# Two pairs' A12 block products remade as seven inner quarter products in the projection stage of a hybrid attention block

## The chip, the core and the metric

The kernel runs on one core of a Trainium2 chip. The metric is device time in microseconds for one execution. TensorE (PE) does the matmuls; its weight loads (PEld) overlap them. VectorE (DVE), ScalarE (ACT) and GpSimd (POOL) work on tiles in SBUF, DVE and ACT also on PSUM; SyncE (SP) issues most transfers. Each engine takes its instructions in program order.

## What is computed

One layer of a block with three parallel mixers. Nearly all of its arithmetic is matrix products in float32 with a model width of 1024 and 1024 tokens:

```python
h = rms_norm(x, g_pre)
a_qkv, bq, bk, bv, mq, ga, gb, gm, mg = split(h @ w_in)   # w_in: 1024 x 10496 columns
aq, ak = rope(a_qkv[0], pos), rope(a_qkv[1], pos)         # dilated windows, 3 groups of 8 heads
...                                                       # three attentions
ya = (oa * silu(ga)) @ w_br_a                             # and yb, ym
gates = sigmoid(mg + b_merge)
out = (gates[0] * ya + gates[1] * yb + gates[2] * ym) @ w_out
x + rms_norm(out, g_post)
```

The change lies in the part of `h @ w_in` that makes the rotated queries and keys of the dilated attention (`aq`, `ak`), some of the SiLU gates, and the merge gates (`mg`).

## The kernel before

**Precision.** A float32 operand is held as two tiles, a high part (`h`) that ACT rounds to PE's format and a low part (`l`) that DVE computes as the difference; the helper `split` (lines 90 to 92) does both. A product of two operands is three matmuls: high by high, high by low, low by high. In the matmul rows of the profile, 128*128 is the weight tile and 128x512 the moving one.

**Pairs and blocks.** The stage around line 1370 takes two units of 128 output columns at a time, called a pair: 27 pairs, numbered by `n` in the order of `PAIRS` (line 1097): rope units and others (three of SiLU gates, twelve of merge gates) in turn, so that pairs 0, 2, ... 22 are rope, 1, 3, 5 gates, and 7, 9, ... 23, 24, 25, 26 merge. The 1024 inner dimension and the 1024 tokens are each halved, and the two units are the third halving: a pair is a 2 by 2 block product, which the kernel makes with seven block products instead of eight, after Strassen and Winograd. The blocks of the weights are A11, A12 (first unit: first and second half of the inner dimension), A21, A22 (second unit) and four sums of them, S1 to S4; those of the tokens are B11 to B22 and four sums T1 to T4. `PRODUCTS` (line 954) says which goes with which:

```python
PRODUCTS = (("A11","B11"), ("A12","B21"), ("S2","T2"), ("S3","T3"), ("S4","B22"), ("S1","T1"), ("A22","T4"))
```

Each block product is 12 matmuls of 128x512 (four inner chunks by three terms), in `pair_product`. The tokens' blocks are made before the stage and lie in tiles `hh`, `hl` and others; the weights' sums are made on POOL by `k_sum` (S1, S2, S3, S4 are its `j` 1, 2, 3, 4, in three tiles `SF`, named vot, vot, vgt), and split by `k_block` into four tiles vS in turn. A11 and A12 are split together by `k_own` into one pair of tiles `OWN` (wh, wl), 1024 columns wide.

**What follows a product.** Products accumulate in PSUM: X (A11, then S2, S3, A22 on top), W (S1, then S4) and Y (A12). Between them ACT copies X out (`keep_copy`: after A11 to `p1`, after S2 to `v_`, after S3 to `y_`), so a later product into X has to wait for the copy. `c_add` adds a PSUM bank and such a copy on DVE, which gives a quarter of the pair's result: unit `u`, token half `t`. `c_fin` scales it (merge, gate: one DVE operation and later, by `behind`, Tanh on ACT and a store) or multiplies it by cosine and sine (rope: two DVE operations); `turn_it` combines rope results on POOL into tiles ko (L1213, L1214), and `k_store` stores them.

**Order.** It is written out by hand in the loop over `n` (lines 1458 to 1529): PE runs, for each pair, S2(n), S1(n), S3(n), A11(n+1), A22(n), A12(n+1), S4(n), and behind each product stand the DVE, ACT, POOL and DMA instructions that are issued with it. Each engine keeps this order and waits only for data and for tiles that come free. `k_load` loads a unit's weights (512 KB, on SP) two pairs ahead. The stage before (line 1340) makes the values of the third group in the same block form with 128x256 matmuls; its side work stands in the table `SIDE`, whose keys are its 28 steps.

Of the kernel before, what the change touches and what calls it, by code (L numbers as in the profile page):

```python
# [33 lines left out]
def block(ctx: ExitStack, tc: tile.TileContext, x, xT, memT, cst, msk, bcst, tabA, gpost,  # L34
# [224 lines left out]
    wos = dram.tile([3, 4, P, S], F32, name="wos")  # L259

# [911 lines left out]
    def c_fin(n, u, t, ps_=None):  # L1172

        r = RV.pop((n, u, t)) if ps_ is None else kr() if n < last else p1
# [107 lines left out]
    for n in range(28):  # L1282
# [34 lines left out]
        if k == 3:  # L1317
            left += [lambda i=i, j=j, b=now[j]: v_evac(i, j, b) for j in range(4)]

    SIDE = {2: [lambda: v3_sum("S2", "A22", "S3", OP.subtract, v3.tile([P, 1024], F32, name="xS2"))],  # L1320
# [41 lines left out]
    close(v3p)  # L1362
    kpp, kp = pool("kp")
    p1, v_, y_ = [vb.tile([P, 512], F32, name=x) for x in ("vv2", "vv3", "vrt")]
    SPARE = [wp.tile([P, 1024], F32, name=x) for x in ("wh", "wl")]
# [4 lines left out]
    def pair_product(n, an):  # L1370
# [5 lines left out]
        for k in range(4):  # L1376
            bh, bl = k_tokens(TOKENS[an], k)
            for q, (a, b) in enumerate(((ah[:, k], bh), (ah[:, k], bl), (al[:, k], bh))):
                PE.matmul(BANK[n, c], a, b, start=k == 0 and q == 0 and not more, stop=k == 3 and q == 2,  # L1379
                          skip_group_check=c in "XW")  # L1380

# [76 lines left out]
    for n in range(last + 1):  # L1458
        N = n + 1
        pair_product(n, "S2")  # L1460
        c_add(*((n - 1, 0, 1, BANK[n - 1, "W"], v_) if n else (0, 0, 0, BANK[0, "Y"], p1)))
        behind()
        k_block(n, "A22")
        if n == last:
            y_load(1)
        if n:
# [7 lines left out]
        behind()  # L1474
        if n < last:
            k_own(N)
        if n:
# [6 lines left out]
        pair_product(n, "S3")  # L1484
        behind()
# [4 lines left out]
        if n + 2 <= last:  # L1490
            k_load(n + 2, 0)
        if n == last - 1:
            op_load(lo)
        c_fin(n, 0, 0)
# [4 lines left out]
        behind()  # L1499
        if n < last:  # L1500
# [37 lines left out]
    behind()  # L1538
    close(kpp)
# [900 lines left out]
```

## Time and profile before

| | |
|---|---|
| median of 3 runs | 1362.17 us (1361.77 to 1362.71) |
| the profiled execution | 1362.23 us, span 1360.5 us |
| PE busy | 98% of the span, granted clock 0.998 |
| DVE, ACT, POOL busy | 74%, 48%, 43% |
| DMA | 213.84 MB, mean 157 GB/s |
| pair stage | 527.1 to 1041.7 us of the span, 2268 matmuls |

A row of the profile begins with a line of the kernel, the engine and the operation; then come the tiles written and read, with numbers left out, and shapes. In rows in order of time the first two numbers are start and duration in microseconds, and brackets at the end give idle time of the engine just before and what ended it. The idle time of an engine that is not the bound costs nothing by itself.

### The profile page before, as it was taken

How to read it: one execution, taken by the hardware profiler on the slowest of the kernel's cores; microseconds unless marked ns; L12 is line 12 of the kernel's file. 1: busy time of each engine (PE TensorE's matmuls, PEld its weight loads, DVE VectorE, ACT ScalarE, POOL GpSimd, SP SyncE). 2: the span in 40 equal slices, each digit the busy share in tenths (PEclk: the TensorE clock that was granted, in tenths of full speed). 3: DMA queues.
4: the chain of work that ended last, by engine and by line, in shares of the span. 5: the costliest groups of instructions: out<-in, count | busy, mean ns of one | idle time of the engine just before them, and what ended most of it. 6: DMA issues, size and time to landing. Idle time of an engine off the chain costs nothing.

```text
span 1360.5 us, 23348 instructions
## 1 busy us (share of the span) xinstructions
PE 1338.4 (98%) x8567; PEld 1101.6 (81%) x8567; DVE 1011.6 (74%) x1821; ACT 650.4 (48%) x1383; POOL 588.8 (43%) x449
## 2 busy tenths in 40 slices
PE   7999999999999999999999999999999999999997
PEld 7899987767668899888888888888888777778886
DVE  7868677776776877777887766787756666768977
ACT  7544366666654443333334333333345676763332
POOL 0516703778760003455556534565531244662003
PEclk9999999999999999999999999999999999999999
DMA  6356522223157773232333333332256777977455
GB/s 254 109 171 232 180 94 93 82 82 113 62 171 273 241 237 130 85 111 90 124 116 111 122 108 124 117 109 99 90 174 229 248 219 230 274 229 234 145 186 185
DMA packets 124435, 213.84 MB, mean 157 GB/s; under 512 B 31680, under 2 KB 63776, under 8 KB 124320
## 3 DMA queue, kind: packets, MB, share of 16 engines
q1 hardware_dynamic: 115008, 198.42, 44.5%
q10 hardware_dynamic: 9312, 13.93, 2.8%
q8 instruction: 67, 1.10, 0.3%
q14 instruction: 48, 0.39, 0.1%
HBM read 145.92 MB, written 66.38 MB: 156 GB/s over the span
## 4 chain that ended last, share of the span: by engine, by line
PE 91%; DVE 3%; ACT 2%; DMA 1%; issue 1%; POOL 1%; SPq 0%; DVEq 0%; ACTq 0%; POOLq 0%
PE s L1379 38%; PE d L1978 6%; PE s L1290 4%; PE ov L866 4%; PE s L2202 4%; PE sc L2120 3%; PE s L1340 3%; PE s L1653 2%; PE d L133 2%; PE d L131 2%; PE d L129 2%; PE s L848 2%; PE s L849 2%; PE tr L830 2%; PE d L572 2%; PE d L2202 2%
## 5 line engine op out<-in xcount | busy, mean ns | idle before, releaser
L1379 PE MATMUL s<-hh,vS 128*128 128x512 f32 x432 | 141.6, 389 | 0.0
L854 POOL TENSOR_TENSOR bl<-bl,bp 128x512 f32<-128x512 f32 x90 | 118.4, 1316 | 35.3 <-ACT bp L851 29.4
L1379 PE MATMUL s<-vA,vS 128*128 128x512 f32 x486 | 114.5, 389 | 0.0
L92 DVE TENSOR_TENSOR vS<-vot,vS 128x512 fp32r<-128x512 f32 x81 | 92.3, 1141 | 20.1 <-ACT vS L91 20.1
L1379 PEld LDWEIGHTS s<-vA,vS 128*128 128x128 f32 x486 | 91.2, 188 | 18.9
L831 DVE TENSOR_REDUCE bn<-tr 128x1 f32<-128x512 f32 x128 | 83.9, 687 | 23.8 <-PE tr L830 22.5
L851 ACT ACTIVATE bp<-s 128x512 f32<-128x512 f32 x128 | 76.3, 598 | 40.7 <-PE s L849 36.9
L1379 PEld LDWEIGHTS s<-hh,vS 128*128 128x128 f32 x432 | 81.1, 188 | 16.8
L1379 PE MATMUL s<-hh,wl 128*128 128x512 f32 x216 | 84.3, 390 | 0.0
L1379 PE MATMUL s<-hl,wh 128*128 128x512 f32 x216 | 84.1, 389 | 0.0
L1379 PE MATMUL s<-hh,wh 128*128 128x512 f32 x216 | 84.1, 389 | 0.0
L1379 PE MATMUL s<-hl,vS 128*128 128x512 f32 x216 | 84.0, 389 | 0.0
L1665 ACT ACTIVATE pra<-pra,sts 128x192 f32<-128x192 f32 (+1 forms) x176 | 72.4, 415 | 14.5 <-DVE sts L1664 14.2
L1124 POOL TENSOR_TENSOR vot<-wr 128x512 f32<-128x512 f32 x14 | 23.9, 1707 | 117.0 <-DMA wr<-in_wu 115.6
L1383 ACT ACTIVATE vv<-s 128x512 f32<-128x512 f32 x54 | 32.3, 599 | 87.9 <-PE s L1379 55.7
L1664 DVE CUSTOM_DVE_ANT_0 pra<-s,mask 128x192 f32<-128x192 f32 (+1 forms) x192 | 48.8, 309 | 33.6 <-PE s L1653 19.4
L133 PE MATMUL d<-hh,wl 128*128 128x512 f32 x160 | 64.0, 400 | 0.0
L131 PE MATMUL d<-hl,wh 128*128 128x512 f32 x160 | 63.4, 397 | 0.0
L129 PE MATMUL d<-hh,wh 128*128 128x512 f32 x160 | 62.9, 393 | 0.0
L1124 POOL TENSOR_TENSOR vot<-vot,vA 128x512 f32<-128x512 f32 x13 | 20.9, 1609 | 94.0 <-DVE vS L92 94.0
L866 PE MATMUL ov<-bp,VS 128*64 128x256 f32 x512 | 58.8, 382 | 0.0
L91 ACT ACTIVATE vS<-vot 128x512 fp32r<-128x512 f32 x81 | 49.4, 625 | 12.2 <-ACT vy L1191 4.1
(640 smaller groups left out, 4007.4 us busy)
## 6 DMA issues: line engine op xcount, KB each, us to landing
wr<-in_wu SPq DMA_DIRECT2D x38, 512.0 KB
vA<-in_wu SPq DMA_DIRECT2D x26, 512.0 KB
qkd<-ko SPq DMA_DIRECT2D x96, 128.0 KB
wl<-thd SPq DMA_DIRECT2D x24, 512.0 KB
wos<-os SPq DMA_DIRECT2D x12, 512.0 KB
wr<-in_wbr SPq DMA_DIRECT2D x24, 256.0 KB
aq<-qkd SPq DMA_DIRECT2D x12, 512.0 KB
ak<-qkd SPq DMA_DIRECT2D x12, 512.0 KB
```

The source lines that it names most:

```text
L92: V.tensor_tensor(dst_l, src, dst_h.bitcast(F32), op=OP.subtract)
L129: PE.matmul(dst, wh[:, k, :], hh[k][:, t], start=k == 0, stop=False)
L131: PE.matmul(dst, wh[:, k, :], hl[k][:, t], start=False, stop=False)
L133: PE.matmul(dst, wl[:, k, :], hh[k][:, t], start=False, stop=k == 7)
L831: V.tensor_reduce(st[i]["n"][:, j, c:c + 1], s, axis=AX.X, op=OP.min)
L851: A.activation(pp, s, AF.Exp, scale=-1.0)
L854: E.tensor_tensor(lsum[i % 2], d[0] if kt == 1 else lsum[i % 2], pp, op=OP.add)
L866: PE.matmul(o[e * 64:e * 64 + 64, c].rearrange("p (j q) -> p j q", j=2), w, x[:, e], start=kt == 0, stop=kt == NT, skip_group_check=True)
L1379: PE.matmul(BANK[n, c], a, b, start=k == 0 and q == 0 and not more, stop=k == 3 and q == 2, skip_group_check=c in "XW")
L1665: A.activation(src, src, AF.Exp, scale=-1.0, bias=bias, accum_out=sts[:, 1, h, T:T + 1])
L1978: PE.matmul(ps_, a, b, start=k == 0 and q == 0, stop=k == 3 and q == 2)
L2202: PE.matmul(dst[:, e[0]:e[1]], a, b, start=k == 0 and q == 0, stop=k == 3 and q == 2)
```

## The change

The second weight block times the first token half of the second half of the inner dimension, A12 by B21, leaves the sequence of single pairs. Pairs (1, 2), (3, 4) to (25, 26) are taken together: their two A12 blocks, stacked, are a matrix of 256 output columns by 512, B21 is 512 by 512 tokens, and this product is itself made by seven inner products of quarter blocks in the same scheme, each of six 128x256 matmuls (`q_product`). Only pair 0 keeps its own A12 product.

- PE: 312 matmuls of 128x512 go, 546 of 128x256 come. In an odd pair the inner A11, A12 stand behind S2, the inner S2 behind S3, the inner S1 behind A22; in the even pair behind it the inner S3 stands behind S2, the inner A22 and S4 behind S1. They accumulate in two PSUM banks of another pool and one of the stage's.
- DVE: seven `q_add` per two pairs add the 256-column results from PSUM into `P1[0]` and `P1[1]`, copies of X after A11; the first quarters of both pairs (`c_fin(.., 0, 0)`) are finished together in the even pair, and their two `c_add` go. `k_own` splits 512 columns; the other half of `OWN` holds A12 of the odd pair's inner blocks, split by `k_own_second` in the even pair ahead, and then inner S3 and A22, split by `q_last`. `q_blocks` splits the inner S1, S2, S4 into tiles na and nb.
- POOL: `q_sums`, four 256-column sums per two pairs, behind `k_sum(N, 2)`.
- SP: `q_load`, four loads of 512 KB per two pairs of the token sums (two tiles nt in turn). `k_load(n + 2, 0)` stands earlier in the loop.
- Ahead of the stage, steps 3 to 17 of the stage at line 1340 get `QUARTER_STEPS`: four loads of xT, four scalings on ACT, eight sums, four splits on ACT and POOL, four stores to a new DRAM tensor `tqd`.
- `c_add(n, 1, 1)` stands ahead of A22(n) and `behind` after `k_own`. The program is built with a smaller scratch for descriptors, which frees SBUF.

On DVE, from the scaled quarter of the even pair 8 to the add that frees W's copy. vS tiles are blocks of weights, s and d PSUM, tab the rope tables, vy, vv, wh, wl results in spare tiles. Before:

```order
L1170 TENSOR_TENSOR vv_7199<-s_7126,vrt 128x512
L1197 TENSOR_TENSOR vy_7215<-s_7026,tab_5514 128x512
L1198 TENSOR_TENSOR vv_7214<-s_7026,tab_5515 128x512
L92 TENSOR_TENSOR vS_7218<-vot,vS_7218 128x512
L1170 TENSOR_TENSOR vy_7233<-s_7201,vv_5954 128x512
L92 TENSOR_TENSOR vS_7235<-vot,vS_7235 128x512
L92 TENSOR_TENSOR vS_7238<-vgt,vS_7238 128x512
L1170 TENSOR_TENSOR wh<-s_7126,vv_5955 128x512
```

and now:

```order
L92 TENSOR_TENSOR wl<-vA_7183,wh 128x512
L1176 TENSOR_TENSOR vy_7414<-s_7341,vrt 128x512
L1203 TENSOR_TENSOR vy_7443<-s_7233,tab_5515 128x512
L1204 TENSOR_TENSOR vv_7442<-s_7233,tab_5516 128x512
L92 TENSOR_TENSOR vS_7446<-vot,vS_7446 128x512
L92 TENSOR_TENSOR na<-vy_7419,na 128x512
L92 TENSOR_TENSOR nb<-vv_7420,nb 128x256
L92 TENSOR_TENSOR vS_7465<-vot,vS_7465 128x512
L92 TENSOR_TENSOR vS_7468<-vgt,vS_7468 128x512
L1176 TENSOR_TENSOR vy_7502<-s_7341,vv_5993 128x512
```

The add for the quarter (0, 0) of pair 9 is gone from between S2(9) and S1(9), two inner splits stand there instead, and the second half of `OWN` is split ahead of the add.

On POOL, the same period: sums into vot and vgt for the blocks of pair 9 (and the next pair's first), and the two turns of pair 8 into ko. Before:

```order
L1124 TENSOR_TENSOR vot<-vot,vA_7023 128x512
L1124 TENSOR_TENSOR vot<-vA_7023,vot 128x512
L1213 TENSOR_TENSOR ko_7242<-vy_7166,vv_7214 128x16x32
L1214 TENSOR_TENSOR ko_7243<-wl,vy_7215 128x16x32
L1124 TENSOR_TENSOR vot<-wr 128x512
```

and now:

```order
L1125 TENSOR_TENSOR vot<-vot,vA_7183 128x512
L1439 TENSOR_TENSOR vy_7419<-wr 128x256
L1440 TENSOR_TENSOR vy_7419<-vy_7419,vA_7183 128x256
L1441 TENSOR_TENSOR vv_7420<-vA_7183,vy_7419 128x256
L1442 TENSOR_TENSOR vv_7420<-vA_7183,wr 128x256
L1125 TENSOR_TENSOR vot<-vA_7183,vot 128x512
L1219 TENSOR_TENSOR ko_7472<-wl,vv_7442 128x16x32
L1220 TENSOR_TENSOR ko_7473<-wl,vy_7443 128x16x32
```

The four quarter sums stand between the sum for S2(9) and the sum for S4(9).

The diff, cut to its core:

```diff
+    tqd = dram.tile([4, P, S], F32, name="tqd")
...
-        split(h, l, KR[n, 0])
+        t = slice(0, 512 if n else S)
+        split(h[:, t], l[:, t], KR[n, 0][:, t])
...
+    def k_own_second(n):
+        h, l = OWN
+        split(h[:, hi], l[:, hi], KR[n, 0][:, hi])
...
+    def q_load(nm):
+        nc.sync.dma_start(q_tile(nm).bitcast(F32), tqd[int(nm[1]) - 1])
...
+    def q_sums(a):
+        x, y = QS[a] = [kr(), kr()]
+        G.tensor_tensor(x[:, 0:256], rows_at(a + 1, 0), rows_at(a + 1, 1), op=OP.add)
+        G.tensor_tensor(x[:, 256:512], x[:, 0:256], rows_at(a, 0), op=OP.subtract)
+        G.tensor_tensor(y[:, 0:256], rows_at(a, 1), x[:, 256:512], op=OP.subtract)
+        G.tensor_tensor(y[:, 256:512], rows_at(a, 0), rows_at(a + 1, 0), op=OP.subtract)
+
+    def q_blocks(a):
+        x, y = QS[a]
+        split(NX[0][:, 0], NX[0][:, 1], x)
+        split(NX[1][:, 0, 0:256], NX[1][:, 0, 256:512], y[:, 0:256])
+
+    def q_last(a):
+        h, l = OWN
+        split(h[:, 768:1024], l[:, 768:1024], QS.pop(a)[1][:, 256:512])
+        split(h[:, 512:768], l[:, 512:768], rows_at(a + 1, 1))
...
+        for k in range(2):
+            m = slice(128 * k, 128 * k + 128)
+            bh, bl = b[k]
+            for q, (u, x) in enumerate(((w[0][:, m], bh), (w[0][:, m], bl), (w[1][:, m], bh))):
+                PE.matmul(QB[c], u, x, start=first and k == 0 and q == 0, stop=k == 1 and q == 2, skip_group_check=True)
+
+    def q_add(z, t, c):
+        x = P1[z][:, 256 * t:256 * t + 256]
+        V.tensor_tensor(x, QB[c], x, op=OP.add)
...
+        one, two, ahead = n % 2 == 1, n > 0 and n % 2 == 0, N % 2 == 1 and n < last
         pair_product(n, "S2")
+        if one:
+            q_product("A11")
+            q_product("A12")
         c_add(*((n - 1, 0, 1, BANK[n - 1, "W"], v_) if n else (0, 0, 0, BANK[0, "Y"], p1)))
+        if one:
+            q_add(0, 0, "X")
+            q_add(0, 0, "Y")
+        elif two:
+            q_add(1, 1, "W")
+            q_product("S3")
+            q_add(1, 1, "X")
         behind()
         k_block(n, "A22")
...
+        if n + 2 <= last:
+            k_load(n + 2, 0)
...
         pair_product(n, "S1")
         keep_copy(v_, n)
-        behind()
+        if two:
+            q_product("A22")
+            q_product("S4")
+            q_add(1, 0, "X")
+            q_add(0, 1, "W")
         if n < last:
             k_own(N)
+        behind()
...
         pair_product(n, "S3")
+        if one:
+            q_product("S2")
+            q_add(0, 1, "X")
+            q_load("T3")
...
-        c_fin(n, 0, 0)
+        if not n:
+            c_fin(n, 0, 0)
+        elif two:
+            for z in range(2):
+                c_fin(n - 1 + z, 0, 0, P1[z], P1[z] if n == last else None)
+        if ahead:
+            k_own_second(N)
...
+        c_add(n, 1, 1, BANK[n, "W"], y_)
...
+        if one:
+            q_last(n)
+        if ahead:
+            q_sums(N)
+            for nm in ("T2", "T1"):
+                q_load(nm)
         pair_product(n, "A22")
         if n < last:
-            keep_copy(p1, N)
-        c_add(n, 1, 1, BANK[n, "W"], y_)
+            keep_copy(P1[N % 2 == 0], N)
...
-        pair_product(N, "A12")
+        if one:
+            q_product("S1")
+            q_load("T4")
         c_fin(n, 1, 0, BANK[n, "X"])
         k_block(N, "S2")
+        if ahead:
+            q_blocks(N)
...
         pair_product(n, "S4")
-        c_add(N, 0, 0, BANK[N, "Y"], p1)
...
-    nc = bacc.Bacc("TRN2", target_bir_lowering=False, num_devices=1)
+    nc = bacc.Bacc("TRN2", target_bir_lowering=False, num_devices=1, dynamic_dma_scratch_size=1024)
```

More of the change, by code (lines that the diff above doesn't have):

```diff
@@ L1170, in c_add, with c_fin @@
         V.tensor_tensor(r, ps_, z, op=OP.add)
[L1172 to L1174 removed]
+    def c_fin(n, u, t, ps_=None, r=None):
+        r = RV.pop((n, u, t)) if ps_ is None else r or (kr() if n < last else SF[1])
         src = r if ps_ is None else ps_
@@ L1329, in block @@
             26: [lambda: k_block(0, "S2")], 27: [lambda: k_block(0, "S1"), lambda: k_block(0, "S3"), lambda: k_sum(0, 4)]}
+    QUARTER_STEPS = {3: [lambda: [q_source(i) for i in range(4)]], 5: [lambda: [q_scale(i) for i in range(2)]],
+                     6: [lambda: [q_scale(i) for i in range(2, 4)]], 7: [lambda: q_sub("T3", "B22", "B12")],
+                     8: [lambda: q_sub("T1", "B12", "B11")], 9: [lambda: q_split("T3")],
+                     11: [lambda: q_sub("T2", "B22", "T1")], 12: [lambda: q_split("T1")],
+                     14: [lambda: q_sub("T4", "B21", "T2")], 15: [lambda: q_split("T2")], 17: [lambda: q_split("T4")]}
     for n in range(28):
@@ L1353, in block @@
         for f in SIDE.get(n, ()):
+            f()
+        for f in QUARTER_STEPS.get(n, ()):
             f()
@@ L1380, in pair_product, with rows_at, q_product @@
                           skip_group_check=c in "XW")
+    def rows_at(n, z):
+        return KR[n, 0][:, 512 + 256 * z:768 + 256 * z]
+    QS = {}
+    def q_sums(a):
[12 more added lines that the diff above has]
+        split(h[:, 512:768], l[:, 512:768], rows_at(a + 1, 1))
+    QB = {}
+    def q_product(an):
+        i = ("S1", "S2", "S4").index(an) if an in ("S1", "S2", "S4") else None
+        if i is None:
+            c = 512 if an in ("A11", "A22") else 768
+            w = [x[:, c:c + 256] for x in OWN]
+        else:
+            w = [NX[0][:, z, 256 * i:256 * i + 256] if i < 2 else NX[1][:, 0, 256 * z:256 * z + 256] for z in range(2)]
+        bn = TOKENS[an]
+        if bn[0] == "T":
+            t = TQ[bn].rearrange("p (x k q) -> p x k q", x=2, k=2)
+            b = [(t[:, 0, k], t[:, 1, k]) for k in range(2)]
+        else:
+            kk, t = 2 + 2 * int(bn[1]), slice(256 * int(bn[2]) - 256, 256 * int(bn[2]))
+            b = [(hh[kk + k][:, t], hl[kk + k][:, t]) for k in range(2)]
+        c = "Y" if an == "A12" else "W" if an in ("S1", "S4") else "X"
+        first = an in ("A11", "A12", "S1")
+        if first:
+            QB[c] = (pss1() if c == "Y" else psd())[:, 0:256]
+        for k in range(2):
+            m = slice(128 * k, 128 * k + 128)
[5 more added lines that the diff above has]
+        V.tensor_tensor(x, QB[c], x, op=OP.add)
     def keep_copy(dst, n):
@@ L1489, in block @@
             k_sum(N, 3)
-        if n + 2 <= last:
-            k_load(n + 2, 0)
         if n == last - 1:
             op_load(lo)
-        c_fin(n, 0, 0)
+        if not n:
+            c_fin(n, 0, 0)
+        elif two:
+            for z in range(2):
+                c_fin(n - 1 + z, 0, 0, P1[z], P1[z] if n == last else None)
+        if ahead:
+            k_own_second(N)
         if n == last:
@@ L1538, in block @@
     behind()
+    close(nqp)
     close(kpp)
```

34 lines of the change are left out of this document (30 added, 4 removed).

## Prediction

> **What bounds the kernel now.** I read the shares of the engines first, then the chain that ended last, then the pair stage by windows, then the order of time of DVE, POOL and ACT in one period of it. From the page:
>
> ```profile
> PE 1338.4 (98%) x8567; PEld 1101.6 (81%) x8567; DVE 1011.6 (74%) x1821; ACT 650.4 (48%) x1383; POOL 588.8 (43%) x449
> PE 91%; DVE 3%; ACT 2%; DMA 1%; issue 1%; POOL 1%; SPq 0%; DVEq 0%; ACTq 0%; POOLq 0%
> ```
>
> PE is the bound nearly everywhere. Two windows price a matmul (length, PE busy and count, PEld, clock, DMA share); the third is one period of two pairs with all engines (PE, PEld, DVE, ACT, POOL). Below them stand the first and last matmul of the pair stage, and what PE's weight loads waited for in it (us, times).
>
> ```profile
> 527.10:1041.70 514.60, 514.60 (x2268) 425.15 (x2268) 1.00 0.36 117
> 486.70:527.10 40.40, 40.35 (x336) 40.28 (x336) 1.00 0.62 199
> 674.00:712.10 38.10, 38.10 (x169) 31.38 (x168) 30.30 (x31) 14.27 (x22) 21.34 (x12) 1.00 0.35 111
> 527.06 0.40 PE L1379 MATMUL s<-hh,wh 128*128 128x512 f32 x1
> 1041.38 0.39 PE L1379 MATMUL s<-hh,vS 128*128 128x512 f32 x1
>   DVE wl L92: 0.8, 4
> ```
>
> A 128x512 matmul costs 514.60/2268 = 0.2269 us, a 128x256 one in the stage before 40.35/336 = 0.1201 us. A product of a pair is 12 matmuls, 2.72 us; product number k of the stage (A11(0) is 0, then A12(0), then seven per pair) starts at 527.06 + 2.7225k. So A11(9) is product 61 and starts at 693.14, A22(8) ends at 698.58, S2(9) starts at 704.0, S3(9) at 709.5. PE hardly waits, yet DVE has only 38.1 - 30.3 = 7.8 us idle in a period, and the one wait shown is for a DVE split: DVE is close behind.
>
> **The change: PE.** 26 A12 products leave, 26 x 12 x 0.2269 = 70.8 us. 13 x 7 inner products of six 128x256 matmuls come, 546 x 0.1201 = 65.6 us. The difference is -5.2 us, -0.40 per period. The 256-wide rate is measured with a new weight load for each matmul, as here, and PEld was busy all the time there too (40.28 of 40.40), so I see no further bound.
>
> The Trainium skill (TensorE: Matmul & The Clock Gate, Back-to-back issue gap) gives N/2.4 + 2.5 ns for the isolated gap, 215.8 and 109.2 ns, and by that the saving would be an estimated 7.7 us. The rows' two rates are slower, so the sum goes by them.
>
> **The change: what must now be hidden.** Per period DVE gets seven 256-wide PSUM adds for two 512-wide ones, seven splits (four of 512, three of 256 columns) for two of 1024; POOL gets four 256-wide sums; ACT the high halves; SP four 512 KB loads. The question is when, so I walk one period, the even pair 8, a rope pair, in the clock of before. DVE, before (start, duration, what it waited for):
>
> ```profile
> 691.02 1.23 DVE L92 TENSOR_TENSOR wl<-vA,wh 128x1024 fp32r<-128x1024 f32 x1 [2.26 <-ACT wh L91]
> 692.17 0.69 DVE L1178 TENSOR_TENSOR vy<-vy,rb 128x512 f32<-128x512 f32 x1
> 694.73 0.69 DVE L92 TENSOR_TENSOR vS<-vot,vS 128x512 fp32r<-128x512 f32 x1 [1.87 <-ACT vS L91]
> 695.34 0.69 DVE L1197 TENSOR_TENSOR vy<-wl,tab 128x512 f32<-128x512 f32 x1
> 696.06 1.67 DVE L1198 TENSOR_TENSOR wl<-wl,tab 128x512 f32<-128x512 f32 x1
> 697.65 0.68 DVE L1170 TENSOR_TENSOR vv<-s,vrt 128x512 f32<-128x512 f32 x1
> 698.80 0.69 DVE L1197 TENSOR_TENSOR vy<-s,tab 128x512 f32<-128x512 f32 x1 [0.48 <-PE s L1379]
> 699.41 0.68 DVE L1198 TENSOR_TENSOR vv<-s,tab 128x512 f32<-128x512 f32 x1
> 700.01 0.68 DVE L92 TENSOR_TENSOR vS<-vot,vS 128x512 fp32r<-128x512 f32 x1
> 701.52 0.69 DVE L1170 TENSOR_TENSOR vy<-s,vv 128x512 f32<-128x512 f32 x1 [0.83 <-PE s L1379]
> 702.13 2.50 DVE L92 TENSOR_TENSOR vS<-vot,vS 128x512 fp32r<-128x512 f32 x1
> 704.55 2.57 DVE L92 TENSOR_TENSOR vS<-vgt,vS 128x512 fp32r<-128x512 f32 x1
> 707.04 0.68 DVE L1170 TENSOR_TENSOR wh<-s,vv 128x512 f32<-128x512 f32 x1
> ...
> 711.17 1.22 DVE L92 TENSOR_TENSOR wl<-wr,wh 128x1024 fp32r<-128x1024 f32 x1
> ```
>
> POOL in the same period, the two turns of pair 12 (another dilation group), and the mean of a 256-wide POOL operation:
>
> ```profile
> 695.57 1.61 POOL L1124 TENSOR_TENSOR vot<-vot,vA 128x512 f32<-128x512 f32 x1 [7.35 <-DVE vS L92]
> 700.77 1.29 POOL L1124 TENSOR_TENSOR vot<-vA,vot 128x512 f32<-128x512 f32 x1 [3.59 <-DVE vS L92]
> 702.02 2.06 POOL L1213 TENSOR_TENSOR ko<-vy,vv 128x512 f32<-128x512 f32 x1
> 704.02 2.55 POOL L1214 TENSOR_TENSOR ko<-wl,vy 128x512 f32<-128x512 f32 x1
> ...
> 778.24 1.29 POOL L1213 TENSOR_TENSOR ko<-vy,wh 128x512 f32<-128x512 f32 x1
> 779.48 1.74 POOL L1214 TENSOR_TENSOR ko<-vv,wl 128x512 f32<-128x512 f32 x1
> ```
>
> ```profile
> L356 POOL TENSOR_TENSOR qn<-t1b,ssb 128x256 f32<-128x256 f32 x16 | 10.8, 678 | 1.3
> ```
>
> ACT:
>
> ```profile
> 692.94 0.72 ACT L1191 ACTIVATE vy<-vy,cs 128x512 f32<-128x512 f32 x1 [1.95 <-DVE vy L1178]
> 693.69 0.33 ACTq L1192 DMA_DIRECT2D thd<-vy  x1
> 694.06 0.63 ACT L91 ACTIVATE vS<-vot 128x512 fp32r<-128x512 f32 x1 [0.40 <-ACT vy L1191]
> ...
> 707.82 0.60 ACT L1383 ACTIVATE vv<-s 128x512 f32<-128x512 f32 x1 [2.94 <-DVE wh L1170]
> ```
>
> The reader should see that a split of SBUF operands takes 0.61 us to the next start when POOL is idle (700.01), but 2.50 and 2.57 us beside the turns: it started at 702.13, POOL's turn ended at 704.08, it ended 0.55 us later; and POOL's next operation in turn got longer by that. The two take turns, whole operations at a time; operations that read PSUM (707.04) stay at 0.6. The SBUF — State Buffer page of the Trainium skill (Who interferes with whom) says the same, an exclusive lock for a whole instruction; by it the new POOL sums, all SBUF to SBUF, speak against this change.
>
> The walk after. The last inner product in front of S3(8), S4, ends one product ahead of A11(9), at 690.41; DVE, in order, waits for it with its add, so it is idle until 690.63 (0.22 behind the end, as 698.80 behind 698.58). Add 0.34, half split of the next pair 0.6, scaling of pair 7 at 691.57 (before 692.17). From that scaling to the S4 split lie 2.56 us, as in before (692.17 to 694.73: Tanh, its store, the high half, all on ACT): 694.13. Then in queue order, POOL in brackets: split 694.73; the scaling of pair 7 that moved here, 695.4; [sum for S2(9), 1.16, that is 1.61 less its wait for DVE]; first rope operation of pair 8; [quarter sum 0.58, my estimate from 0.68 and half of 1.16]; second rope operation; [quarter sum]; second half of the OWN split: 699.4; PSUM add 699.95; two PSUM rope operations 701.17 (before 700.01); S2(9) split 701.8. S2(9) now starts one product earlier than before, at 701.3, its low block is used 0.23 later: 0.35 us late.
>
> Next, two inner-block splits with [S2(9) released, sum 1.2] between them: 703.9; [turn 2.0], S1(9) split 706.4; [turn 2.0], S3(9) split 708.9; the W add 709.6; the copy of X on ACT 0.7, as from 707.04 to 708.42 in before: 710.3. S3(9) on PE may not start before that copy. PE's own way to S3(9) from 698.58 is S4, S2, two inner products and S1, 9.6 us: 708.2. So S3(9) waits 2.1 us, the 0.35 included. The margin in before was 709.5 - 708.4 = 1.1. The first half of OWN for A11(10) ends about 713.6 and is needed at 714.0 behind that wait: covered.
>
> Bounds: if no POOL operation held DVE here, the walk is shorter by 1.16 + 1.16 + 1.2 + 4.0 = 7.5 us and the wait is nothing; if every one of the four quarter sums and both sums for pair 10 held it too, 3.5 us more, a wait of 5.6. I take 2.1, since the rows show the alternation exactly. The rest is nearer zero: in the odd pair the same walk ends some 0.5 us ahead of PE; the quarter sums of tokens in the stage before (POOL about 10 us more) lie beside DVE that is idle at 494 to 516 and splits that are used microseconds later: 0, if that cover fails about 1 us; four loads more raise the DMA share from 0.35 by about 2 MB in 38 us, 55 GB/s beside 111: 0. Two loads wait on SP for inner products, with the stores of the rotated tiles behind them; these have a period's time. The inner products accumulate in two banks that this stage leaves idle and in one of its six; before took three new ones per pair, now five per two pairs.
>
> **Sum.** Pairs 4, 6, 8, 10, 16, 18, 20, 22 have the long turn: 8 x 2.1 = 16.8. Of these pairs 4 and 6 also have a gate's extra DVE pass in the moved steps: 2 x 0.6 = 1.2. Pairs 2, 12, 14 have the short turn (1.2 each, 1.6 us less): 3 x 0.5 = 1.5. The last two periods have no turn: 0. With PE's -5.2: +14.3. The profiled execution took 1362.23 us (span 1360.5), 0.06 above the median of 1362.17: 1376.5.
>
> **Rivals.** The gain arrives: PE stays full, 1362.2 - 5.2 = 1357. For it: PE waited only 0.8 us in 514.6, and DVE has 7.8 us of idle time per period. It needs the walk to S3(9) to be 2.1 us shorter, for instance if one turn of 2.0 us ran while DVE reads PSUM; from there on the time is below before. Against it: that walk is a single chain in queue order, and the margin of before was 1.1 us while PE's way there got 1.3 us shorter.
>
> Half of it: the quarter sums run beside PSUM operations only and the 0.35 and 1.2 us fall away, leaving 0.9 us in eight periods, 1362.2 + 7 - 5 + 1 = 1365, just slower.
>
> DVE becomes the bound of the whole period: 30.3 + 7 of new work and POOL's 2.6 us of sums, against 37.7 of PE; with the upper bound of 5.6 us in eight periods, 1362 + 45 - 5 = 1402. The idle time at 690 speaks against it.
>
> Late token quarters (T3, T4 are loaded only after the inner product before has let go): some 9 us from issue to use, for one 512 KB load at 111 GB/s and more; a late microsecond in 12 periods gives 1369.
>
> **Chances.** Walk as above (1370 to 1385) 0.51; gain 0.19; half 0.19, of which a third within the resolution; DVE bound 0.07; late loads 0.04. About 0.2% is what a measurement can tell from no change (1359.4 to 1364.9). Faster 0.18, same 0.08, slower 0.74. The likeliest case's own range is 1370 to 1385; the range to hold eight in ten goes from the gain, 1356.5, to 1386.
>
> **What would show it.** Right: PE waits in the even pairs ahead of S3, for ACT's copy, behind the DVE add on W; DVE splits of 1.5 to 2.6 us beside POOL; the 256-wide matmuls at 0.120 us; periods near 39.8 us with long turns, near 38.2 with short ones. Wrong: periods of 37.7 us without waits, or waits for the loads of the token quarters, or a 256-wide rate above 0.13 us, which alone would eat the gain.

## The result, and the profile after

The changed kernel took **1397.32 us** (median of 4, 1396.45 to 1399.87) against 1362.44 (1361.77 to 1362.97) for the kernel before beside it: ratio 1.0259, 95% interval 1.0244 to 1.0275. Slower, as forecast, but by 34.9 us where +14.3 was forecast, and above the range of 1356.5 to 1386. The profiled execution of after took 1399.87 us, its span 1398.0. The shares of the engines and the chain that ended last, from the page of after:

```profile
PE 1346.6 (96%) x8801; PEld 1111.9 (80%) x8801; DVE 1084.9 (78%) x1951; ACT 668.4 (48%) x1456; POOL 651.0 (47%) x513
PE 44%; DVE 14%; ACT 2%; DMA 2%; issue 1%; POOL 0%; ACTq 0%; DVEq 0%; POOLq 0%
```

PE's share of the chain fell from 91% to 44%, DVE's rose from 3% to 14%. PE's own waits in the two stages, longest first (engine, line, whom it waited for: us, times, longest). L1382 is the stage ahead of the pairs, L1429 a pair's product, L1176 `c_add`, L1485 `keep_copy` (in other kernels these numbers differ a little):

```profile
PE s L1429 <- DVE vy L1176: 7.8, 6, 2.4
PE s L1382 <- ACT wh L91: 5.1, 2, 4.6
PE s L1429 <- DVE wl L1176: 5.1, 3, 2.5
PE s L1429 <- ACT vv L1485: 4.4, 6, 3.1
PE s L1429 <- DVE wh L1176: 3.8, 2, 2.5
PE s L1382 <- DVE wl L92: 2.3, 3, 1.1
```

So there are two losses: one in the stage ahead, which had no such wait, and one in the pairs, mostly for `c_add` and not for ACT's copy. By windows (length; busy time and count of PE, PEld, DVE, ACT, POOL; clock; DMA share; GB/s) the two stages and one long-turn period of two pairs, from S4(8) to S4(10):

```profile
487.40:538.00 50.60, 43.17 (x338) 42.02 (x338) 29.36 (x36) 20.08 (x31) 12.75 (x13) 0.93 0.65 206
538.00:1079.80 541.80, 518.96 (x2505) 432.44 (x2504) 458.58 (x550) 210.29 (x376) 313.47 (x209) 0.99 0.49 163
725.21:764.92 39.71, 38.25 (x186) 31.86 (x186) 35.09 (x41) 15.32 (x28) 25.28 (x17) 1.00 0.48 159
```

The stage ahead took 50.6 us where it had taken 40.4, the pair stage 541.8 where it had taken 514.6: 10.2 and 27.2, together 37.4 of the 37.5 by which the span grew. In order of time, the wait in the period of pair 10 (PE), with DVE, ACT and POOL around it:

```profile
764.92 0.50 PE L1429 MATMUL s<-hh,vS 128*128 128x512 f32 x1 [1.30 <-DVE vy L1176]
756.41 0.69 DVE L1184 TENSOR_TENSOR vy<-vy,rb 128x512 f32<-128x512 f32 x1
758.99 0.69 DVE L92 TENSOR_TENSOR vS<-vot,vS 128x512 fp32r<-128x512 f32 x1 [1.89 <-ACT vS L91]
759.60 0.68 DVE L1184 TENSOR_TENSOR vy<-vv,rb 128x512 f32<-128x512 f32 x1
760.20 1.78 DVE L1206 SCALAR_TENSOR_TENSOR vv<-nc,tab 128x512 f32<-128x512 f32 x1
761.91 1.22 DVE L1207 SCALAR_TENSOR_TENSOR vv<-nc,tab 128x512 f32<-128x512 f32 x1
763.05 1.22 DVE L92 TENSOR_TENSOR wl<-vA,wh 128x512 fp32r<-128x512 f32 x1
764.19 0.68 DVE L1176 TENSOR_TENSOR vy<-s,vrt 128x512 f32<-128x512 f32 x1
768.62 2.56 DVE L92 TENSOR_TENSOR vS<-vot,vS 128x512 fp32r<-128x512 f32 x1
773.57 0.68 DVE L1176 TENSOR_TENSOR wl<-s,vv 128x512 f32<-128x512 f32 x1
757.20 0.72 ACT L1197 ACTIVATE vy<-vy,cs 128x512 f32<-128x512 f32 x1 [3.02 <-DVE vy L1184]
758.32 0.63 ACT L91 ACTIVATE vS<-vot 128x512 fp32r<-128x512 f32 x1 [0.40 <-ACT vy L1197]
759.83 1.60 POOL L1125 TENSOR_TENSOR vot<-vot,vA 128x512 f32<-128x512 f32 x1 [7.57 <-DVE vS L92]
763.80 1.05 POOL L1441 TENSOR_TENSOR wh<-vA,vy 128x256 f32<-128x256 f32 x1
```

S4(10) accumulates on W, so it may not start before `c_add(n, 1, 1)` has read W (764.19). In before A12 of the next pair, 2.72 us, stood between A22 and S4 and covered that; now nothing does. Ahead of the add DVE stood idle for 1.89 us: the split for S4 wants ACT's high half (758.32), ACT is in order and first does the tanh of pair 9 (757.20), and that wants DVE's product (756.41). The walk I had forecast is otherwise there.

### The profile page after: what moved, and what is told of

Same layout as the page of the kernel before. It is cut to its first block, busy times and chain, and to the rows that moved or that the text cites. A ratio compares the mean times of both kernels' runs of the same rounds, so it can differ in the third digit from the quotient of the medians.

```text
span 1398.0 us, 24177 instructions
## 1 busy us (share of the span) xinstructions
PE 1346.6 (96%) x8801; PEld 1111.9 (80%) x8801; DVE 1084.9 (78%) x1951; ACT 668.4 (48%) x1456; POOL 651.0 (47%) x513
## 3 DMA queue, kind: packets, MB, share of 16 engines
q8 instruction: 69, 1.13, 0.3%
## 4 chain that ended last, share of the span: by engine, by line
PE 44%; DVE 14%; ACT 2%; DMA 2%; issue 1%; POOL 0%; ACTq 0%; DVEq 0%; POOLq 0%
PE s L1429 19%; PE d L2116 6%; DVE vS L92 4%; PE s L2340 4%; PE d L1478 3%; PE sc L2258 3%; PE s L1791 2%; PE d L2340 2%; DVE wl L92 2%; PE tr L1857 1%; PE tr L1825 1%; DVE nb L92 1%; DMA tqd<-nt 1%; DVE vy L1184 1%; ACT vS L91 0%
## 5 line engine op out<-in xcount | busy, mean ns | idle before, releaser
L1429 PE MATMUL s<-hh,vS 128*128 128x512 f32 x432 | 144.5, 396 | 18.1 <-DVE vy L1176 7.8
L855 POOL TENSOR_TENSOR bl<-bl,bp 128x512 f32<-128x512 f32 x90 | 118.8, 1320 | 34.9 <-ACT bp L852 29.0
L1429 PE MATMUL s<-vA,vS 128*128 128x512 f32 x486 | 119.8, 393 | 1.6 <-ACT vv L1485 1.3
L1429 PEld LDWEIGHTS s<-hh,vS 128*128 128x128 f32 x432 | 81.8, 189 | 40.4 <-DVE vy L1176 10.4
L1429 PEld LDWEIGHTS s<-vA,vS 128*128 128x128 f32 x486 | 88.2, 188 | 21.1 <-ACT vv L1485 5.0
L832 DVE TENSOR_REDUCE bn<-tr 128x1 f32<-128x512 f32 x128 | 84.0, 687 | 24.7 <-PE tr L831 23.3
L92 DVE TENSOR_TENSOR vS<-vot,vS 128x512 fp32r<-128x512 f32 x81 | 86.5, 1074 | 21.3 <-ACT vS L91 21.3
L1429 PE MATMUL s<-hl,vS 128*128 128x512 f32 x216 | 84.7, 392 | 0.0
L1485 ACT ACTIVATE vv<-s 128x512 f32<-128x512 f32 x41 | 24.5, 598 | 100.1 <-PE s L1429 32.1
L92 DVE TENSOR_TENSOR wl<-wr,wh 128x1024 fp32r<-128x1024 f32 (+2 forms) x39 | 50.2, 1287 | 22.8 <-ACT wh L91 22.8
L91 ACT ACTIVATE vS<-vot 128x512 fp32r<-128x512 f32 x81 | 50.6, 626 | 11.6 <-ACT vy L1197 3.7
L849 PE MATMUL s<-QH,KS 128*128 128x512 f32 x128 | 52.6, 411 | 1.5 <-ACT bp L852 1.5
L867 PEld LDWEIGHTS ov<-bp,VS 128*64 128x64 f32 x512 | 35.3, 137 | 21.9 <-issue 5.4
L831 PE MATMUL tr<-KS,QH 128*128 128x512 f32 x128 | 52.3, 408 | 0.1
```

Source lines behind the costliest of these rows:

```text
L92: V.tensor_tensor(dst_l, src, dst_h.bitcast(F32), op=OP.subtract)
L832: V.tensor_reduce(st[i]["n"][:, j, c:c + 1], s, axis=AX.X, op=OP.min)
L855: E.tensor_tensor(lsum[i % 2], d[0] if kt == 1 else lsum[i % 2], pp, op=OP.add)
L867: PE.matmul(o[e * 64:e * 64 + 64, c].rearrange("p (j q) -> p j q", j=2), w, x[:, e], start=kt == 0, stop=kt == NT, skip_group_check=True)
```

## The experiments

Each run stood beside runs of the kernel before on the same chip, whose medians were 1362.0 to 1362.8. Theory at the start: the preparation costs the stage ahead 10 us by order; in the pairs DVE's walk, lengthened by POOL, costs the rest; PE's saving is real and covered up.

### The preparation: no_prep and prep_alone

```diff
-    QUARTER_STEPS = {3: [... q_source ...], 5: [... q_scale ...], ... 17: [lambda: q_split("T4")]}
+    QUARTER_STEPS = {3: [lambda: [nc.sync.dma_start(tqd[i], xT[4 + i]) for i in range(4)]]}
```

prep_alone is the other half: the steps stay, the loop over pairs is that of before.

> The kernel after without the token quarters' preparation in the stage of 128x256 values: no loads of the four tokens' halves, no scaling, differences and splits there; four copies from DRAM to DRAM fill the tensor that the pair stage loads the quarters from (so their values are left out). The pair stage is untouched. Theory (the preparation alone costs the 10 us by which the value stage grew, since ACT and POOL do their old splits behind it): the value stage goes back from 50.6 to about 41 us, the pair stage stays near 541 (539 to 542), the time is about 1387 (1385 to 1390). Rival (the value stage is late because the tables, loads and pools of the changed stage come late, whatever is prepared): 1395 to 1398.

> The kernel before's pair stage with the kernel after's preparation of token quarters in the stage ahead of it; nothing reads the quarters. Theory: before plus the preparation's cost, 1362 + 10 = 1372 (1370 to 1376; the first pair's weights are loaded late too). Rival 1 (ACT and POOL hide it, as the prediction had it): 1362 to 1363. Rival 2 (the cost of 10 us comes from the changed pair stage reaching back into it): 1362 to 1365.

no_prep: **1384.03** (ratio to before 1.0160, 1.0143 to 1.0177), 13.3 less than after. prep_alone: **1377.06** (1.0109, 1.0094 to 1.0124), 15.0 more than before. Both halves agree: some 13 to 15 us, just past both theories (1385 to 1390 and 1370 to 1376), since the first pair waits too; the rivals (hidden beside the stage, or caused by the changed pairs) are out. From after, ACT, POOL and, in the first pair, PE:

```profile
502.55 1.38 ACT L1340 ACTIVATE na<-na,cs 128x512 f32<-128x512 f32 x2 [6.08 <-DMA na<-in_xT]
509.53 0.80 PE L1382 MATMUL s<-wh,vA 128*128 128x256 f32 x2 [4.65 <-ACT wh L91]
520.87 0.74 POOL L1349 TENSOR_TENSOR nt<-nb,nt 128x256 f32<-128x256 f32 x1 [6.66 <-DMA tqd<-nt]
522.35 0.63 ACT L1353 ACTIVATE nt<-nt 128x512 fp32r<-128x512 f32 x1 [8.04 <-POOL nt L1349]
546.75 0.96 PE L1429 MATMUL s<-aq,vS 128*128 128x512 f32 x3 [3.14 <-ACT vv L1485]
```

ACT stands 6.08 us at a scaling whose operand is still being loaded, with the splits of the stage queued behind it; then POOL stands 6.66 us for a store that must free a tile, and ACT 8.04 us for POOL. In no_prep none of these waits is left; its pair stage, 1065.5 - 527.6 = 537.9 us, is still 23.3 longer than before's, and its span 22.5.

### The addition on W ahead: add_first2 and best1

```diff
-        for z in range(2): c_fin(n - 1 + z, 0, 0, P1[z], ...)
-        if ahead: k_own_second(N)
...
         c_add(n, 1, 1, BANK[n, "W"], y_)
+        for z in range(2): c_fin(n - 1 + z, 0, 0, P1[z], ...)
+        if ahead: k_own_second(N)
```

best1 also moves `q_blocks(N)` into the next pair and the preparation to later steps. A first form of the edit, add_first, which also took the tiles in the new order, deadlocks and has no time.

> The kernel after with one change of order on DVE: in each even pair the addition on W, for which S4 of that pair waits, is put ahead of the rope, gate and merge products of the inner results and ahead of the split of the own block's second half (buffers are handed out in the old order). Theory (two waits of like length one behind the other): S4's wait goes, worth 1.6 us by starts of matmuls where the profile shows 1.30 idle and 2.8 where it shows 2.45; in periods with long turns DVE still comes to the next addition on W at the old time (773.57 in the period of pair 10), so the wait ahead of S3 of the next pair takes its place (1.5 to 2.1 us) and they gain 0 to 0.5 each; the three periods with gates and the two or three with short turns gain all of it; in all 9 to 15 us, 1382 to 1388. Rival 1 (the addition's place is the whole loss): every period 37.8 to 38.2, some 21 us, 1374 to 1379. Rival 2 (DVE's walk from split to split sets every period): 1395 to 1398.

> Three edits on the kernel after, the whole computation: the addition on W ahead as in the run beside it; the splits of the quarter sums moved out of the stretch between S2's and S1's splits into the next pair's turn (behind the split of A22), so that DVE comes about 2 us earlier to the addition on W ahead of S3; and the quarter tokens scaled about nine block steps later, with the stores issued by ACT two to three steps behind the splits instead of by SP. Theory: both waits go, periods of 37.8 to 38.4 and a pair stage of 512 to 518 us; the preparation keeps 0 to 4 of its 13 us; 1360 to 1370. Rival (DVE and POOL share a port over the whole walk, so the splits cost the same wherever they stand): periods stay at 39 or more in long turns, pair stage 525 or more, 1372 to 1385. A time below 1358 is looked for by neither.

add_first2: **1395.24** (1.0243, 1.0228 to 1.0259), 2.1 less than after: my theory of two waits in a row had the long turns right and the rest wrong; rival 2 had the time. PE in the period of pair 10 of add_first2:

```profile
764.47 0.50 PE L1429 MATMUL s<-aq,vS 128*128 128x512 f32 x1 [0.15 <-DVE vS L92]
772.72 1.45 PE L1429 MATMUL s<-vA,vS 128*128 128x512 f32 x5 [1.17 <-ACT vv L1485]
```

The wait ahead of S4 is gone, and exactly the two waits of the prediction stand in its place: S2 for its split, S3 for ACT's copy. The period is 39.93 us, against 39.71. best1: **1385.98** (1.0172, 1.0157 to 1.0187); the stage ahead was free of waits, but the first pair waited 4.50 us and the long-turn period from 716.65 to 756.36 was 39.71 again, now with 1.3 to 1.4 us ahead of A11 for the own split. Its theory (1360 to 1370) missed; its rival had the periods of 39 or more. Three orders, nearly one length (39.71, 39.93, 39.71): these two moves changed the place of PE's wait and not the period.

### The sums on POOL left out: no_sums

```diff
-        G.tensor_tensor(x[:, 0:256], rows_at(a + 1, 0), rows_at(a + 1, 1), op=OP.add)
...
-        split(NX[0][:, 0], NX[0][:, 1], x)
+        split(NX[0][:, 0], NX[0][:, 1], KR[a, 0][:, hi])
```

> The kernel without the quarter tokens' preparation, and with the quarter sums on POOL left out too: the inner weights are split from rows of the own blocks instead, as many splits of the same size, so the numbers are others. Theory (POOL's sums beside DVE lengthen the rope product from 0.7 to 1.78 and 1.22 and the own split from 0.68 to 1.22 us, which is what makes the addition on W late): S4's wait falls from 1.30 to 0 to 0.5, and the time from 1384 to 1370 to 1376. Rival (the number and order of DVE's instructions makes it late, the sums beside it nothing): the wait stays above 1.0, 1381 to 1385.

**1368.73** (1.0044, 1.0029 to 1.0058), 15.3 less than no_prep and just below the theory's 1370 to 1376, with waits ahead of S4 of 0.21 to 0.26 outside the gates (1.30 in no_prep) and 0.83 to 0.84 at them (2.45). So in this order 52 sums of about 1 us cost 15 us. How, the same two instructions show: first POOL's sums in after beside the rope product at 761.91 and the own split at 763.05 (rows above), then the product and the split in no_sums:

```profile
761.40 1.18 POOL L1439 TENSOR_TENSOR vy<-wr 128x256 f32<-128x256 f32 x1
762.66 1.06 POOL L1440 TENSOR_TENSOR vy<-vy,vA 128x256 f32<-128x256 f32 x1
739.15 0.68 DVE L1207 SCALAR_TENSOR_TENSOR vv<-nc,tab 128x512 f32<-128x512 f32 x1
739.76 0.68 DVE L92 TENSOR_TENSOR wl<-vA,wh 128x512 fp32r<-128x512 f32 x1
```

Beside the sums both take 1.22 us, without them 0.68: together 1.08 us, the amount by which the wait ahead of S4 fell. The rope product ahead of them keeps its 1.8 us in no_sums (1.78 at 760.20 in after), since the sum beside it is one that the kernel before has too; the theory had counted it among the gains. The addition at 764.19, with a PSUM bank as one operand, takes 0.68 beside a quarter sum. The Trainium skill (SBUF — State Buffer, Who interferes with whom) has DVE with two SBUF inputs and a POOL instruction that reads SBUF hold a shared pair of ports for a whole instruction each; these rows agree.

### The split ahead of the tanh: late_tanh, best2, best3

```diff
+        if two: k_block(n, "S4")
         behind()
-        k_block(n, "S4")
+        if not two: k_block(n, "S4")
```

> The kernel after with one change of order in each even pair: the split for S4 is put ahead of the tanh of the merge (or gate) that ACT runs there, so that DVE no longer stands idle 1.9 us ahead of that split (758.99 in the period of pair 10) while ACT's copy waits behind the tanh and the tanh behind a product on DVE. Theory (in the kernel after DVE's walk from that split on is without a gap until the next pair's inner products, 34 us, then waits for PE and ACT some 4 us and closes the period of 39.7; a gap taken out of it shortens the period, whichever wait PE shows): periods with long turns fall by 1.3 to 1.7, with gates by 1 to 2; ten to twelve of them; 1379 to 1386. Rival 1 (PE's waits are what counts and another takes the place, as with the addition put ahead): 1393 to 1397. Rival 2 (POOL starts its sums earlier too and the collisions grow): less than 5 us, 1392 to 1397.

> The whole computation: the split for S4 ahead of the tanh as in the run beside it, and the quarter tokens prepared late: scaled about nine block steps later, the second difference kept in a buffer of its own so that no difference waits for a store, stores issued by ACT some four steps behind. Theory: the preparation keeps 0 to 3 of its 13 us, and the time is that of the run beside it less 10 to 13: 1367 to 1375. Rival (what the preparation costs is not the order but ACT's, POOL's and the DMA's time): 1376 or more.

> As the run beside it, and with the addition on W ahead of the rope, gate and merge products as well. Theory (once DVE's walk is shorter than the period, the place of the addition counts): 1362 to 1370, up to 5 us less than without it. Rival (the walk still sets the period): within 2 us of the run beside it.

late_tanh: **1387.53** (1.0182, 1.0167 to 1.0198), 9.8 less than after, just short of the 11 to 18 that the theory's 1379 to 1386 amounts to: the gates did not gain. By windows one long-turn period of late_tanh, then DVE and PE:

```profile
733.43:772.02 38.59, 37.98 (x186) 31.92 (x186) 35.38 (x41) 15.22 (x28) 25.28 (x17) 1.00 0.51 164
755.18 0.68 DVE L92 TENSOR_TENSOR vS<-vot,vS 128x512 fp32r<-128x512 f32 x1
760.39 0.68 DVE L1176 TENSOR_TENSOR vy<-s,vrt 128x512 f32<-128x512 f32 x1
772.02 1.65 PE L1429 MATMUL s<-vA,vS 128*128 128x512 f32 x6 [0.62 <-ACT vv L1485]
642.70 0.80 PE L1429 MATMUL s<-hh,vS 128*128 128x512 f32 x1 [2.40 <-DVE wl L1176]
```

The gap of 1.89 us ahead of the split is gone, all that stands behind it on DVE comes earlier, the addition on W too, and the period is 1.1 shorter. Putting the addition alone earlier had left the period as it was, so what set it was the walk DVE, ACT, DVE, and the gap was a piece of it.

best2 (as late_tanh, the preparation later, and a third tile for it): **1375.28** (1.0094, 1.0079 to 1.0109), 12.3 less than late_tanh with the same preparation done: its cost was its order. best3 (as best2, the addition ahead): **1372.49** (1.0073, 1.0058 to 1.0088). The same edit that had been worth 2.1 was worth 2.8, within the up to 5 I allowed, but the time is above the theory's 1362 to 1370: its rival, within 2 us, is not far off.

### PE's sequence alone: pe_adds, adds_first, pe_alone, pe_tanh

These leave out what feeds the inner products: quarter sums, their splits, quarter tokens (pe_alone and pe_tanh the additions of their results as well).

```diff
-            w = [NX[0][:, z, 256 * i:256 * i + 256] if i < 2 else ... for z in range(2)]
+            w = [x[:, 512:768] for x in OWN]
```

> The inner products and their additions without what feeds them: left out are the quarter sums, their splits, the quarter tokens' preparation and loads, and the weights and tokens of the seven inner products are parts of blocks that are there already; the own block is split whole as before. PE runs the kernel after's sequence. Theory (PE's saving of 5.2 us is real and is lost only to what DVE and POOL do beside it): periods of 37.7 to 37.9, the time 1357 to 1360. Rival 1 (the order of products on PE alone, with S4 right behind A22, makes the wait for the addition on W, whatever DVE has to do): periods above 38.5, 1366 to 1375. Rival 2 (256-wide matmuls cost more than counted): periods of 38.1 without any wait, 1362.

> The kernel of inner products and additions alone (quarter sums, their splits, quarter tokens left out) with the addition on W put ahead on DVE as above. Theory: the wait ahead of S4 (0.71 in long and short periods, 1.39 at the gates) is DVE's order, not ACT's copy nor PE's, and goes; what stays is the wait for the own block's split in some periods (0.3 to 0.45); periods of 37.7 to 38.2, and PE's saving shows at last: 1358 to 1364. Rival (S4 stands too close behind S3 for the copy and the addition, whatever their order): unchanged, 1375 to 1378.

> PE's sequence of the kernel after alone: left out are the additions of the inner results, the quarter sums, their splits, and the quarter tokens' preparation and loads; the inner products take weights and tokens that are there already. Theory (312 matmuls of 512 columns out, 546 of 256 columns in, 0.40 us less in a period of two pairs): periods of 37.7, 1356 to 1359. Rival 1 (the missing product between A22 and S4 alone makes S4 wait for the addition on W): periods of 38.1 and more, 1361 to 1370. Rival 2 (256-wide matmuls cost more than 0.1201 us between other products): 1361 to 1363 without any wait.

> The kernel of PE's sequence alone (additions of the inner results, quarter sums, their splits and the quarter tokens left out) with the split for S4 put ahead of the merge's tanh, as in the run late_tanh. In the run of PE's sequence alone every even pair still waited 0.70 to 0.71 (gates 1.39) ahead of S4, DVE 1.83 idle for ACT's copy behind the tanh. Theory (that idle 1.8 us of DVE was all that kept PE's 0.40 us a period from showing): waits of 0 to 0.1 outside the gates, long and short periods of 37.7 to 37.9; 1357 to 1362. Rival 1 (S4 so close behind S3 waits whatever DVE's order): periods of 38.8 and more, 1371 to 1376. Rival 2 (the inner products take more than 0.1201 us a matmul between others): periods of 38.1 to 38.3 without a wait, 1362 to 1365.

They gave **1376.92**, **1374.70**, **1375.50** and **1366.88** (ratios 1.0109, 1.0087, 1.0095 and 1.0036): my theory missed all four. PE waited ahead of S4 in pe_adds and pe_alone, for the own block's split in adds_first and pe_tanh; three such rows, from pe_alone, adds_first and pe_tanh (L1424 is a pair's product here, L1469 an inner one):

```profile
744.75 0.50 PE L1424 MATMUL s<-hh,vS 128*128 128x512 f32 x1 [0.71 <-DVE vy L1175]
759.06 0.38 PE L1469 MATMUL d<-hh,wl 128*128 128x256 f32 x1 [1.04 <-DVE wl L92]
753.75 0.39 PE L1469 MATMUL d<-hh,wl 128*128 128x256 f32 x1 [0.66 <-DVE wl L92]
```

So without A12 between A22 and S4 even this lighter walk of DVE comes late as long as it stands in the order of after, and rival 1 of pe_adds (1366 to 1375) was nearer than my theory. That PE's order costs time by itself these runs do not show: best4 below keeps it and has no wait in most periods. These kernels also split the whole own block behind inner A22, which the kernel after does not, so their last waits are partly their own. They could not show what PE saves; the next runs could.

### DVE's walk in the order of what is due: best4, best5, best7

In an even pair, best4 on top of best3:

```diff
+        c_fin(n - 1, 0, 0, P1[0], *slots[0])
         c_add(n, 1, 1, BANK[n, "W"], y_)
+        behind()
+        c_fin(n, 0, 0, P1[1], *slots[1])
...
+        k_block(N, "S2")
+        if ahead: k_own_second(N)
         c_fin(n, 1, 0, BANK[n, "X"])
-        k_block(N, "S2")
...
-        for nm in ("S1", "S3"): k_block(N, nm)
+        k_block(N, "S1")         # S3's split now behind the c_add of the next pair
```

> The whole computation, best3 with DVE's walk put in the order of what is due: in an even pair S4's split, the product for the first inner result, the addition on W, the tanh or gate, then the second inner result's products; S2's split ahead of the own block's second half and of the rope products for the accumulated bank; S3's split behind the next addition on W instead of ahead of it; the splits of the last two quarter tokens behind the first pair's sums. Theory (best3's waits were of order: 0.71 to 0.89 ahead of S3 for ACT's copy behind that addition, 0.44 to 1.27 at the gates, 1.85 in the first pair): 1361 to 1367. Rival (DVE beside POOL fills the period of 38.67, so the waits only move): 1370 to 1374. Below 1358, the content of PE, neither looks.

> The whole computation, best4 with its four waits taken one by one: in the three gate periods S1's split ahead of the rope products and the quarter splits (PE waited 1.50 twice there), the last two quarter tokens' splits behind ACT's copy in the first pair (0.92), the last pair's output splits behind S4's split (0.86). Theory (PE's saving is whole once no order of DVE, ACT or POOL holds it up: periods of 37.70 instead of 38.10, 5 us): 1356 to 1359.5. Rival (the waits move on to the next product): 1360 to 1363, with as many us of waits at other places.

> The whole computation, best5 with two more changes of order on DVE for the three gate periods, which took 39.8 us in best5 against 37.7 of the others (4.6 us in all): the gates' sums behind S1's split instead of ahead of S2's, and, in every odd pair, the split of the next own block ahead of the accumulated bank's rope products, since PE waited 0.99 for it twice. Theory (the gate periods' waits are DVE's order like the rest): gate periods of 37.7 to 38.7, 1356.5 to 1359.5. Rival (in gate periods DVE's work beside POOL does not fit into 37.7 us): gate periods stay above 39, 1360.5 to 1362.

best4: **1362.20** (1.0002, 0.9992 to 1.0011), 10.3 less than best3, within the theory's 1361 to 1367, level with before. A period in the middle of its pair stage, inner A11 to inner A11:

```profile
707.27:744.97 37.70, 37.70 (x188) 31.93 (x186) 33.71 (x41) 15.14 (x27) 24.95 (x17) 1.00 0.53 167
```

PE is busy for all of it, and it is 37.70 us where before had 38.10: this is the predicted saving of 0.40, with every sum, split and load in place. What held the rest stood at two gate periods (1.50 us twice) and at the ends (0.92, 0.86). best5, with these taken on: **1361.66** (0.9993, 0.9984 to 1.0002); the ends are clean, but its periods run 37.67, 38.11, 39.77, 39.84, 37.71 and so on: the waits of the gates only moved, as its rival had it. best7, with the gates' own sums later still: **1364.56** (1.0011, 1.0002 to 1.0020), gate periods of 40.9. There I found no order that fits; the theories of best5 and best7 (1356 to 1359.5 and 1356.5 to 1359.5) missed, and best7 lies above its rival too.

### Inner products except around the gates: mixed

```diff
+    def inner(n):
+        return n > 0 and n not in (3, 4, 5, 6)
...
+        if n < last and not inner(N):
+            pair_product(N, "A12")
```

> The whole computation, best5 with the pairs 3 to 6, around the gates, done as in the kernel before (a whole product and no inner ones), the other twenty-two pairs with inner products. Theory (the walk of DVE does not fit only where the gates' sums come on top; periods of 37.7 elsewhere): the two periods of 39.8 become 38.1, some 3.4 us less than best5 in all, 1357 to 1359.5, and by 2 to 4 us below the kernel before. Rival (the change from one way to the other costs a wait at each end, or the gates collide with the next pairs' sums): 1360 to 1363.

**1359.05** (1357.44 to 1362.56) against 1362.03; ratio **0.9979**, 0.9969 to 0.9988: a version faster than the kernel before, by 3.0 us or 0.2%, within the theory's 1357 to 1359.5. Its eleven double pairs at 0.40 each would give 4.4. Apart from one wait of 0.36 us no matmul of the pair stage waits:

```profile
706.27:743.93 37.66, 37.66 (x187) 31.95 (x186) 33.67 (x41) 15.13 (x27) 24.92 (x17) 1.00 0.52 168
672.26 1.65 PE L1433 MATMUL s<-vA,vS 128*128 128x512 f32 x6 [0.36 <-ACT vv L1489]
```

## Why the prediction was right or wrong

**PE, -5.2 us: right by the period.** The inner matmuls start 0.12 us apart in after, and the periods of best4 and mixed, 37.70 and 37.66, are the count 144 x 0.2269 + 42 x 0.1201 = 37.7. In after the saving lies under waits, and no run shows the whole 5.2: mixed, with eleven of the thirteen double pairs, gained 3.0.

**Token quarters, "0, if that cover fails about 1 us": the step that failed most, 13.3 us.** I named idle time of DVE as the cover. The steps are on ACT, POOL and SP, and what they cost is paid by whatever is queued behind them: the scalings behind a load, differences behind a store. best2 did the same work and gave back 12.3 of it. I did not walk these three queues as I had walked DVE's.

**The walk of DVE: the long-turn size right, the place wrong.** Forecast 2.1 us of wait ahead of S3(9), a period near 39.8; measured 39.7 to 39.9 for pairs 8, 10, 16, 18, 20, with 1.30 us ahead of S4 and up to 0.30 ahead of S3. My own walk put the addition on W at 699.4 to 699.95 and S4 at 698.58; I did not see that S4 must wait for it, by these numbers 1.4 us. The size held all the same, and not by luck alone: from the add of inner S4 to the end of the next addition on W my walk had 19.0 us (690.63 to 709.6) and after took 18.7 (755.47 to 774.17), and what PE waits ahead of S4 it need not wait ahead of S3. add_first2 brought out the wait I had described, 1.13 to 1.27 us ahead of S3 (2.1 was too long), with S2 late by 0.15 to 0.17 outside the gates (0.35 forecast).

**Short turns, 0.5 each, and gates, 0.6 each: mis-sized.** Periods from S4(n) on in no_prep, where the preparation does not disturb them:

| pair n | 2 | 4 | 6 | 8 | 10 | 12 | 14 | 16 | 18 | 20 | 22 |
|---|---|---|---|---|---|---|---|---|---|---|---|
| forecast | 38.2 | 40.4 | 40.4 | 39.8 | 39.8 | 38.2 | 38.2 | 39.8 | 39.8 | 39.8 | 39.8 |
| measured | 42.06 | 42.01 | 39.86 | 39.71 | 39.67 | 39.31 | 39.28 | 39.90 | 39.86 | 39.72 | 38.61 |

The sum is 440.0 against 434.2. The wait ahead of S4 does not ask whether turns are long, so pairs 12 and 14 lose 1.1 more each, and at the gates it was 2.45 us: pair 2, which I had put among the short turns, lost 3.9 more, some 1 us of it, going by pair 4, to PE's clock (last section). Pair 22 lost 1.2 less than forecast: the next even pair, 24, has no rope products in its walk, and the wait ahead of its S4 was 0.16.

**Sum.** Medians: +34.9, of which 13.3 is the preparation and 21.6 the pairs, where I had +14.3. **Rivals.** "Gain arrives" failed in after and is, with less, what mixed does; that it "needs the walk to S3(9) to be 2.1 us shorter" was near the condition, though late_tanh, with 1.9 us taken out, gained only 1.1 a period: the order behind it had to change too. "Half of it" (1365) did not show: no_prep, the pairs alone, is at 1384. "DVE becomes the bound" I gave 0.07 on account of idle time at 690. In after that idle time (1.89 and 1.35 us in the period of pair 10) was part of the loop and no reserve: it was the wait for PE and ACT that closed it. "Late token quarters" did not show: no inner matmul waited for a load.

## What to carry to other kernels

When PE is nearly full and an in-order engine beside it is at 80%, walk each queue that gets an instruction, SP and ACT included, and for every product moved or removed list what its time had covered. If waits move but the period stays, look for a loop over engines and take a gap out of that loop; then put each engine's instructions in the order in which they are due. The same arithmetic took 1397 us in one order and 1362 in another.

## What the runs showed of the hardware

A wait of some 2 us can halve PE's clock behind it. From after, two stretches of 2 us behind the first of its three waits of 2.45 us and one behind the second; from adds_first, a stretch behind a wait of 1.81 us (the clock is the third number from the right):

```profile
602.30:604.30 2.00, 1.93 (x5) 1.55 (x6) 2.00 (x5) 0.35 (x1) 0.12 (x2) 0.51 0.80 236
604.30:606.30 2.00, 2.00 (x7) 1.61 (x6) 2.00 (x3) 0.00 (x0) 2.00 (x2) 0.64 0.98 303
644.35:646.35 2.00, 2.00 (x9) 1.65 (x10) 2.00 (x4) 0.28 (x1) 0.18 (x1) 1.00 0.90 268
638.50:641.90 3.40, 3.40 (x10) 2.62 (x9) 1.86 (x4) 0.00 (x0) 1.99 (x2) 0.50 0.00 0
```

Behind the first, 0.51 and 0.64 were granted, then 1.00; behind the two others of the same length 1.00 throughout. In the two stages, over all kept traces, half the clock was granted behind or during all nine waits of 3.13 us and more, five of the twelve of 2.40 to 2.45 (after, no_prep, late_tanh, best2), three of the four of 1.81 to 1.85 (adds_first, best2, best3), and none of 1.50 or less. It lasted 3.41 us or twice that, and within a trace its beginnings lie whole multiples of 3.41 us apart (506.76, 547.72 and 602.33 in the clock record of after: 12 and 16 times). So where a wait falls on such a grid may decide; that is an inference, and no run tested it. The price: pair 4's period is 42.01 us in no_prep, where half the clock was granted at its start, and 41.00 in after, where it was not, about 1 us. The Trainium skill (TensorE: Matmul & The Clock Gate, HAM oscillation) warns of idle gaps above some 3.4 us; here 1.81 and 1.84 us were enough in adds_first, and 2.45 was not in two cases of three in after.

And a wait costs more than its row says: in pe_alone the idle time is 0.71 us, yet the first matmul behind it starts 1.10 us after the one ahead (743.65 to 744.75), and the next 0.34 later, where 0.23 is the usual distance: 0.98 us in all.
